# Dividing score tiles on ScalarE instead of GpSimd, in a re-ordered program with waits on the shared SBUF port

## The chip, the cores and the metric

The kernel runs on one core of a Trainium2 chip. The metric is the device time of one execution in microseconds (us), the median over several runs. The engines are TensorE (PE in the profile; PEld is its loading of the stationary operand), VectorE (DVE), ScalarE (ACT), GpSimd (POOL) and SyncE (SP). SP only issues DMAs here; POOL computes and also issues the DMAs that add to what lies in SBUF.

## The reference

One layer of a hybrid encoder trunk on x of 512 tokens by 1024 features, in float32:

```
hn  = rms_norm(x);  z = hn @ w_in                       # 1024 x 3590
o_a = 4 heads of differential attention (softmax1 - lam * softmax2) @ v, then a norm
o_b = 6 heads of attention with a cumulative log-forget-gate bias, causal
o_c = 6 heads of chunked attention with a clipped relative-position bias
h   = x + concat(o_a, o_b, o_c) @ w_out                 # 1024 x 1024
u   = causal depthwise conv of width 3 over rms_norm(h) @ w_up     # 1024 x 5632
h   = h + (silu(gate) * val) @ w_down                   # 2816 x 1024
out = h + (p @ w_ple_proj) * sigmoid(rms_norm(h) @ w_ple_gate)
```

All attention heads have 64 columns and norms on queries and keys. A softmax row is exp(s - max) divided by the sum of its exponentials. That division is what the change moves, for the heads of o_b and o_c.

## The kernel before

**Arithmetic.** A float32 product is made of three products of rounded parts: each operand is split into a high part in the format fp32r and a low part, and `mm3` (L511) issues high x high, high x low and low x high. So each weight tile is loaded by SP into `wraw`, copied on ACT to `whi`, and subtracted on DVE (for some tiles on POOL, or by an adding DMA that POOL issues) to give `wlo`. `h`, `Th` and `Tl` hold the residual and the two parts of its transposed, normed form.

**Stages.** First come the eight input projections (`in_unit`, L753), 128 tokens at a time into PSUM banks `z`, and beside them the attention of the head pairs A0, A1, B0 to B2 and C0 to C2. Then the output projection, the up-projection with the convolution (`ff_chain`, L1471), the down-projection, and the gate, whose last products run until the end. Nine of the 22 column blocks of the up-projection and all of the down-projection use a scheme with seven products in place of eight, for which POOL adds or subtracts weights.

**Attention of one head pair.** `split_q` (L715) and `split_k` (L727) turn normed columns by transposes on PE, split them on ACT and DVE, and make three moves of half a tile each on POOL (`move`, L712: `q<-q`, `q<-ql`, `k<-k`). For each head and each block of 128 queries, `softmax_map` (L852) issues two products into a bank `s`; DVE adds the bias, takes the row minimum and writes the tile `e`; ACT takes the exponential with its row sum into `st`; DVE takes the reciprocal of the sum. Then `scores` (L878) finishes the tile. For the A heads POOL scales the second map and DVE combines both. For the B and C heads (6 pairs, 2 heads, 4 blocks: 48 tiles of 128 rows and 128, 256, 384 or 512 columns) one POOL instruction multiplies `e` by the reciprocal in place (L896). `prob_cols` (L902) transposes the finished tiles on PE, and `values` (L930) multiplies them with the values.

**The order of the work.** Nothing is issued where it stands in the source. Between two calls that open and close a plan, each operation becomes an `Op` (L116) with its dependencies (`Plan.add`, L150), a duration (`Plan.price`, L184) and a due time (`Plan.due`, L225). The due time of a PE operation is its place in the PE order plus the number that `SHIFT` (L53) gives its group; those of the other engines follow backwards from what needs them. `Plan.solve` (L236) then plays all five engines against a clock and always picks the free operation that is due first. `emit` (L305) issues the operations in that order, and every engine runs its own in order. There are two plans: one for projections and attention (L595) and one for the rest (L1140).

In the play of L236, an operation on POOL, or one on DVE whose two operands lie in SBUF, is marked `port` (L216), and DVE and POOL exclude each other in such operations (`held`, L245). In the second plan a POOL operation also starts 0.1 us after the DVE operation before it (`late`), and if it is longer than 0.6 us, `emit` gives it a real semaphore wait on that DVE operation (`behind`, L362). DVE never gets such a wait, and in the first plan nobody does. Loads of SP and adding DMAs of POOL share one `wire` in the play, at 0.37 MB/us for SP's and 0.105 for POOL's (L220, L286). PE is kept from mixing single transposes with products (`STICK`, L263).

The lines of this part that matter most:

```
dve.reciprocal(st[:, 2:3], st[:, 1:2])                                          # L873
pool.tensor_scalar(e, e, st[:, 2:3], 1.0, ALU.mult, ALU.mult)                   # L896, B and C heads
if before and op.eng.name == "pool" and before.eng.name == "dve" and op.busy > self.LONG and self.late:
    op.eng.behind(op.ins, before.ins)                                           # L313
```

## Time and profile before

| | us |
|---|---|
| median of 3 runs | 708.28 (708.25 to 709.49) |
| the profiled execution | 707.89 |
| its span, first to last instruction | 706.0 |
| PE busy | 690.3 |
| DVE busy | 552.5 |
| ACT busy | 408.7 |
| POOL busy | 300.6 |

The profile is one execution. Its span is 1.9 us less than the time that was measured for the same execution. In rows of groups the columns are: line, engine, operation, what is written and read with its shapes, the count, busy us, mean ns of one, and the idle time of the engine before them with what ended it. Nearly every row has the line L357, since all operations go through one helper; so the rows are told apart by the names of the tiles. In a table of waits the columns are who waited for what, us in total, times, and the longest. In the chain of waits and the timeline they are the start, the us, and what ran; the timeline adds in brackets how long the engine was idle before and who ended that.

### The profile page before, as it was taken

What the parts mean: (1) busy time and instruction counts of PE and PEld (TensorE: products, weight loads), DVE (VectorE), ACT (ScalarE), POOL (GpSimd) and SP (SyncE); (2) the same over time, 40 slices, a digit from 0 to 9 for tenths busy, and PEclk for the clock granted to TensorE, in tenths of its full rate; (3) what the DMA queues carried; (4) which work ended last, traced back from release to release, by engine and by line L of the source; (5) the groups of instructions that cost most, each with busy time, mean ns of one, the idle gap of its engine ahead of it and who ended that gap; (6) DMA issues with size and microseconds to landing.
All of it is one profiled execution on the core that took longest, in us unless ns stands there. A gap on an engine that the chain in (4) does not pass through costs nothing.

```text
span 706.0 us, 12402 instructions
## 1 busy us (share of the span) xinstructions
PE 690.3 (98%) x4420; PEld 636.4 (90%) x4420; DVE 552.5 (78%) x1126; ACT 408.7 (58%) x781; POOL 300.6 (43%) x403
## 2 busy tenths in 40 slices
PE   7999999999999999999999999999999999999997
PEld 7999999898999888899998999889988888999886
DVE  7679878879788666789888887997877998878722
ACT  6657676565766575666666435665345674536711
POOL 3788677766665452223223334304432203245200
PEclk9999999999999999999999999999999999999999
DMA  9523444423112252584763278651488552204521
GB/s 321 201 83 111 125 117 128 118 60 109 45 61 76 75 124 83 200 244 105 214 159 113 68 186 207 163 162 33 139 211 209 183 168 82 91 32 155 163 85 46
DMA packets 41275, 92.72 MB, mean 131 GB/s; under 512 B 4694, under 2 KB 7510, under 8 KB 41212
## 3 DMA queue, kind: packets, MB, share of 16 engines
q1 hardware_dynamic: 34572, 78.24, 33.1%
q0 software_dynamic: 6352, 13.38, 10.8%
q8 instruction: 35, 0.57, 0.3%
q10 hardware_dynamic: 288, 0.30, 0.1%
q14 instruction: 28, 0.23, 0.1%
HBM read 83.63 MB, written 4.21 MB: 124 GB/s over the span
## 4 chain that ended last, share of the span: by engine, by line
PE 91%; DVE 3%; DMA 2%; ACT 2%; POOL 1%; issue 1%; ACTq 0%; POOLq 0%
PE z L357 46%; PE s L357 22%; PE t L357 16%; PE o L357 7%; DMA wraw<-in_w_up_dram 1%; DVE wlo L357 1%; POOL k L357 1%; POOL q L357 1%; ACT whi L357 1%; DMA zn<-in_w_in_dram 0%; DVE e L357 0%; DVE conv L357 0%; POOL rs L357 0%; ACT e L357 0%; DVE kl L357 0%
## 5 line engine op out<-in xcount | busy, mean ns | idle before, releaser
L357 ACT CAST whi<-wraw 128x768 fp32r<-128x768 f32 (+2 forms) x140 | 106.1, 768 | 59.9 <-POOL wraw L357 11.4
L357 PE MATMUL z<-whi,Th 128*128 128x384 f32 (+2 forms) x356 | 123.4, 351 | 4.5 <-ACT whi L357 4.5
L357 DVE TENSOR_TENSOR wlo<-wraw,whi 128x768 fp32r<-128x768 f32 (+2 forms) x122 | 111.5, 930 | 15.4 <-ACT whi L357 13.6
L357 PE MATMUL z<-wlo,Th 128*128 128x384 f32 (+2 forms) x356 | 123.0, 350 | 0.0
L357 PE MATMUL z<-whi,Tl 128*128 128x384 f32 (+2 forms) x356 | 121.8, 347 | 0.0
L357 PEld LDWEIGHTS z<-whi,Th 128*128 128x128 f32 x356 | 66.9, 189 | 8.0 <-ACT whi L357 4.5
L357 POOL TENSOR_TENSOR wraw<-wraw,wraw 128x256 f32<-128x256 f32 (+1 forms) x22 | 28.3, 1285 | 101.3 <-DVE wlo L357 53.6
L357 PEld LDWEIGHTS z<-wlo,Th 128*128 128x128 f32 x356 | 67.2, 189 | 4.0 <-DVE wlo L357 0.4
L357 PEld LDWEIGHTS z<-whi,Tl 128*128 128x128 f32 x356 | 67.0, 189 | 3.8
L357 ACT ACTIVATE e<-e,st 128x128 f32<-128x128 f32 (+3 forms) x80 | 44.7, 560 | 29.8 <-DVE st L357 29.4
L357 PE MATMUL z<-Th,whi 128*128 128x512 f32 (+1 forms) x156 | 53.2, 346 | 1.4 <-ACT whi L357 1.3
L357 PE MATMUL s<-Th,whi 128*128 128x512 f32 (+1 forms) x156 | 53.3, 345 | 0.6 <-ACT whi L357 0.6
L357 PE MATMUL s<-Th,wlo 128*128 128x512 f32 (+1 forms) x156 | 53.7, 345 | 0.0
L357 PE MATMUL s<-Tl,whi 128*128 128x512 f32 (+1 forms) x156 | 53.6, 345 | 0.0
L357 PE MATMUL z<-Tl,whi 128*128 128x512 f32 (+1 forms) x156 | 53.5, 344 | 0.0
L357 PE MATMUL z<-Th,wlo 128*128 128x512 f32 (+1 forms) x156 | 53.4, 344 | 0.0
L357 POOL TENSOR_TENSOR rs<-rs,nhalf 128x4 f32<-128x4 f32 x40 | 43.5, 1091 | 4.8 <-DVE rs L357 2.3
L357 DVE CUSTOM_DVE_ANT_0 e<-s,bias 128x128 f32<-128x128 f32 (+3 forms) x74 | 33.7, 469 | 12.4 <-PE s L357 7.2
L357 DVE TENSOR_TENSOR conv<-conv,conv 128x512 f32<-128x512 f32 (+1 forms) x31 | 21.0, 691 | 24.0 <-ACT conv L357 23.8
L357 POOL TENSOR_SCALAR e<-e,st 128x512 f32<-128x512 f32 (+3 forms) x48 | 27.2, 576 | 18.1 <-DVE st L357 16.8
L357 PEld LDWEIGHTS z<-Th,whi 128*128 128x128 f32 x156 | 29.1, 188 | 4.8 <-ACT whi L357 1.8
L357 PEld LDWEIGHTS s<-Th,whi 128*128 128x128 f32 x156 | 29.2, 188 | 3.8 <-ACT whi L357 0.8
(352 smaller groups left out, 2152.4 us busy)
## 6 DMA issues: line engine op xcount, KB each, us to landing
wraw<-in_w_up_dram SPq DMA_DIRECT2D x41, 384.0 KB, 4.3
wraw<-in_w_in_dram SPq DMA_DIRECT2D x28, 384.0 KB, 3.7
wraw<-in_w_down_dram SPq DMA_DIRECT2D x16, 384.0 KB, 3.6
whi_again<-in_w_up_dram SPq DMA_DIRECT2D x11, 384.0 KB, 4.5
wraw<-in_w_out_dram SPq DMA_DIRECT2D x16, 256.0 KB, 2.7
wlo_again<-in_w_up_dram SPq DMA_DIRECT2D x10, 384.0 KB, 4.3
wraw<-in_w_up_dram SPq DMA_DIRECT2D x15, 256.0 KB, 4.1
wlo<-wraw POOLq DMA_DIRECT2D x7, 384.0 KB, 4.2
```

The costliest lines, as they stand in the source:

```text
L357: ins = getattr(self.eng, op)(*a, **k)
```

## The change

One line of the computation changes: the 48 tiles of the B and C heads are scaled by ACT (`activation` with `Copy` and a scale per row) instead of POOL. No other instruction is added or taken away, but the order of nearly all of them may differ, as the planner is changed in these ways:

- `SHIFT`, the table of due-time shifts, has new numbers throughout.
- `emit` gives a wait on the other engine's last `port` operation to POOL and to DVE alike, in both plans, for any `port` operation longer than 0.25 us, if the play has it start before the other one's end plus 1.0 us (POOL) or 0.6 us (DVE); a wait on one that the engine already waited for is not repeated.
- In the play POOL starts 0.2 us after DVE's `port` operation and DVE 0.1 us after POOL's.
- SP's and POOL's transfers are played on two wires, at 334 and 164 KB/us alone and 143 and 78 KB/us together, with at most 8 in flight each.
- PE's rule against mixing transposes is gone, and PE prefers operations that have been free for 0.15 us in the first plan (0.1 before) and 0.1 us in the second.
- A tensor named `out_dram` is given regions like a tile's; this kernel declares its output as `out_0_dram`.

```
--- before.py
+++ after.py
@@ -51,44 +51,44 @@
 
 
 SHIFT = {
-    "first": -11.4, "in1_0": -0.3, "in1_1": -25, "in1_2": -2.7, "A0a": -6.5, "in1_3": -12.1, "in2_0": -5.9,
...
+    "first": -8.4, "in1_0": 2, "in1_1": -12, "in1_2": -0.4, "A0a": -5.7, "in1_3": -7, "in2_0": 7.3, "in2_1": 14.9,
...
 }
 
 
@@ -127,15 +127,16 @@
     WRITES = ("out", "accum_out")
     LEAD = {"act": 0.035, "dve": 0.035, "pool": 0.095, "pe": 0.055, "sp": 0.1}
 
-    def __init__(self, clock, there=(), mem=None, fresh=0.0, late=0.0):
-        self.group, self.loaded, self.fresh, self.late = "first", set(), fresh, late
+    def __init__(self, clock, there=(), mem=None, fresh=0.0, sure=0.15):
+        self.sure = sure
+        self.group, self.loaded, self.fresh = "first", set(), fresh
         self.clock, self.there, self.ops, self.mem = clock, [(v.tensor.name, self.region(v), t) for v, t in there], [], mem or {}
 
     @staticmethod
     def region(v):
         size = 2 if v.dtype == BF16 else 4
         (row, pn), *rest = [tuple(x) for x in v.ap]
-        if v.tensor.space == bass.MemoryType.DRAM and v.tensor.name not in STAND_INS:
+        if v.tensor.space == bass.MemoryType.DRAM and v.tensor.name not in STAND_INS and v.tensor.name != "out_dram":
             return 0, 1, v.offset * size, (v.offset + (pn - 1) * row + sum((n - 1) * st for st, n in rest) + 1) * size
         p0, c0 = divmod(v.offset, row)
         return p0, p0 + pn, c0 * size, (c0 + sum((n - 1) * st for st, n in rest) + 1) * size
@@ -186,7 +187,7 @@
         n = self.width(op.outs[0])
         cols = sum(1 for v in op.ins if self.width(v) == 1) - (op.name == "reciprocal")
         acc = "accum_out" in k
-        op.move, op.turns = 0, op.name == "transpose"
+        op.move = 0
         if e == "pe":
             if op.name == "transpose":
                 op.busy = 0.109
@@ -216,9 +217,10 @@
         op.port = e == "pool" and not op.move or e == "dve" and (
             len(here) == len(op.ins) and (op.name == "tensor_scalar" or op.name in ("tensor_tensor", "scalar_tensor_tensor")))
 
-    LONG, STICK = 0.6, 2.0
-    HW, SW, AT_ONCE = 0.37e6, 0.105e6, 8
-    SURE, AHEAD, MUCH, WAIT = 0.1, 1.0, 2.0, 0.6
+    SHORT, HANDED, NEAR = 0.25, {"pool": 0.2, "dve": 0.1}, {"pool": 1.0, "dve": 0.6}
+    RATE = {("sp",): {"sp": 0.334e6}, ("pool",): {"pool": 0.164e6}, ("sp", "pool"): {"sp": 0.143e6, "pool": 0.078e6}}
+    SENT, ARRIVED, AT_ONCE = {"sp": 1.46, "pool": 1.49}, 0.58, 8
+    AHEAD, MUCH, WAIT = 1.0, 2.0, 0.6
     SPARE = {"act": 1.02, "dve": 1.02, "pool": 1.05}
     ENGINES = ("dve", "pe", "act", "pool", "sp")
 
@@ -230,7 +232,7 @@
                 t += op.busy
         for op in reversed(self.ops):
             if op.eng.name != "pe":
-                spent = op.busy + op.lag + 0.05 + (op.move / self.HW + 2.0 if op.move else 0.0)
+                spent = op.busy + op.lag + 0.05 + (op.move / 0.37e6 + 2.0 if op.move else 0.0)
                 op.dl = min([q.dl for q in op.next], default=t) - spent
 
     def solve(self):
@@ -240,11 +242,47 @@
             op.left, op.at = len(op.deps), op.ready + self.LEAD[op.eng.name]
             if not op.left:
                 free[op.eng.name].append(op)
-        wire, out, order = 0.0, {"sp": [], "pool": []}, []
-        turns, alone = False, False
+        wire, now, gate, order = {"sp": [], "pool": []}, 0.0, {"sp": 0.0, "pool": 0.0}, []
         held = {"dve": 0.0, "pool": 0.0}
         other = {"dve": "pool", "pool": "dve"}
-        when = lambda q: max(q.at, held[other[q.eng.name]] + (self.late if q.eng.name == "pool" else 0.0)) if q.port else q.at
+        never = 1e18
+
+        def when(q):
+            if q.port:
+                return max(q.at, held[other[q.eng.name]] + self.HANDED[q.eng.name])
+            if q.move:
+                return max(q.at, gate[q.eng.name]) if len(wire[q.eng.name]) < self.AT_ONCE else never
+            return q.at
+
+        def release(op, e):
+            for q in op.next:
+                q.left -= 1
+                q.at = max(q.at, op.start if e == "pe" and q.eng is op.eng else op.end + self.LEAD[q.eng.name])
+                if not q.left:
+                    free[q.eng.name].append(q)
+
+        def landed(until):
+            nonlocal now
+            while now < until:
+                busy = tuple(e for e in wire if wire[e] and wire[e][0][1] <= now)
+                rate = self.RATE.get(busy, {})
+                step, who = until - now, None
+                for e in wire:
+                    if e in rate and wire[e][0][2] / rate[e] <= step:
+                        step, who = wire[e][0][2] / rate[e], e
+                    if wire[e] and e not in rate and wire[e][0][1] - now < step:
+                        step, who = wire[e][0][1] - now, None
+                now = until if step == until - now else now + step
+                for e in rate:
+                    wire[e][0][2] -= rate[e] * step
+                if who:
+                    op = wire[who].pop(0)[0]
+                    op.end = now + self.ARRIVED
+                    if len(wire[who]) + 1 >= self.AT_ONCE:
+                        gate[who] = op.end
+                    return op, who
+            return None
+
         rank = lambda q: (q.dl, q.pos)
         while True:
             best = None
@@ -253,17 +291,17 @@
                     t = max(clock[e], min(when(q) for q in free[e]))
                     if best is None or t < best[0]:
                         best = t, e
+            there = landed(best[0] if best else never) if wire["sp"] or wire["pool"] else None
+            if there:
+                release(*there)
+                continue
             if best is None:
                 break
             t, e = best
             can = [q for q in free[e] if when(q) <= t]
             if e == "pe":
-                can = [q for q in can if q.at + self.SURE <= t] or can
+                can = [q for q in can if q.at + self.sure <= t] or can
             op = min(can, key=rank)
-            if e == "pe" and op.turns != turns:
-                same = [q for q in can if q.turns == turns and q.dl < op.dl + self.STICK]
-                if same and (turns or sum(q.turns and q.dl < op.dl + self.STICK for q in can) < 2 or min(q.dl for q in same) < op.dl + self.STICK / 2):
-                    op = min(same, key=rank)
             if e not in ("pe", "sp"):
                 soon = [q for q in free[e] if t < when(q) < t + op.busy * self.AHEAD and q.dl < op.dl - self.MUCH]
                 if soon:
@@ -276,16 +314,8 @@
             free[e].remove(op)
             t0 = max(clock[e], when(op))
             busy = op.busy * (1.85 if e == "pe" and t0 < 8.6 else 1.0)
-            if e == "pe":
-                busy += 0.08 * (alone and not op.turns)
-                turns, alone = op.turns, op.turns and not turns
             if op.move:
-                done = out[e]
-                if len(done) >= self.AT_ONCE:
-                    t0 = max(t0, done[-self.AT_ONCE])
-                wire = max(t0 + 2.0, wire) + op.move / (self.HW if e == "sp" else self.SW)
-                op.end = wire + 0.6
-                done.append(op.end)
+                wire[e].append([op, t0 + self.SENT[e], op.move])
             else:
                 op.end = t0 + busy + op.lag
             op.start = t0
@@ -293,11 +323,8 @@
             if op.port:
                 held[e] = t0 + busy
             order.append(op)
-            for q in op.next:
-                q.left -= 1
-                q.at = max(q.at, op.start if e == "pe" and q.eng is op.eng else op.end + self.LEAD[q.eng.name])
-                if not q.left:
-                    free[q.eng.name].append(q)
+            if not op.move:
+                release(op, e)
         assert len(order) == len(self.ops)
         self.last = clock
         return order
@@ -306,13 +333,16 @@
         for op in self.ops:
             for d in op.deps:
                 d.next.append(op)
-        before = None
+        last, known = {"dve": None, "pool": None}, {"dve": None, "pool": None}
         for op in self.choose():
             op.ins = op.eng.now(op.name, [real(v) for v in op.a], {q: real(v) for q, v in op.k.items()})
             if op.port:
-                if before and op.eng.name == "pool" and before.eng.name == "dve" and op.busy > self.LONG and self.late:
-                    op.eng.behind(op.ins, before.ins)
-                before = op
+                e = op.eng.name
+                d = last["pool" if e == "dve" else "dve"]
+                if d and d is not known[e] and op.busy > self.SHORT and op.start < d.start + d.busy + self.NEAR[e]:
+                    op.eng.behind(op.ins, d.ins)
+                    known[e] = d
+                last[e] = op
 
     def choose(self):
         self.due(SHIFT)
@@ -893,7 +923,7 @@
                 pool.tensor_scalar(e2, e2, st2[:, 2:3], X["nlam"], ALU.mult, ALU.mult)
                 dve.scalar_tensor_tensor(e, e, st[:, 2:3], e2, ALU.mult, ALU.add)
             else:
-                pool.tensor_scalar(e, e, st[:, 2:3], 1.0, ALU.mult, ALU.mult)
+                act.activation(e, e, AF.Copy, scale=st[:, 2:3])
             PROB[pr, hh].append(e)
             if hh == 1 and qb == NT - 1:
                 KL_FREE.extend(QK[pr, part][2] for part in range(2) if (pr, part) in QK)
```

## The prediction

> **What bounds the kernel now.** I read the page's busy times first, then the stages, then who PE waited for, then the chain at those places.

> ```profile
> span 706.0 us, 12402 instructions
> PE 690.3 (98%) x4420; PEld 636.4 (90%) x4420; DVE 552.5 (78%) x1126; ACT 408.7 (58%) x781; POOL 300.6 (43%) x403
> ```

> PE is busy for 690.3 of 706.0 us. Matmuls overlap in this trace, so that is no proof that PE runs at its best, but it says that at most 15.7 us of the span are time in which PE does nothing. The table of stages tells where these are (us; PE, PEld, DVE, ACT, POOL busy with counts; clock; DMA share; GB/s).

> ```profile
> 0.00:20.00 20.00, 15.52 (x89) 15.53 (x90) 14.89 (x31) 13.32 (x25) 6.19 (x15) 1.00 0.92 332
> 100.00:150.00 50.00, 47.92 (x293) 45.75 (x292) 41.08 (x139) 31.56 (x79) 36.05 (x50) 1.00 0.37 101
> 150.00:200.00 50.00, 48.94 (x304) 46.48 (x303) 40.42 (x121) 30.86 (x74) 29.77 (x45) 1.00 0.27 84
> 330.00:380.00 50.00, 50.00 (x339) 45.98 (x338) 43.19 (x67) 30.54 (x52) 13.50 (x15) 1.00 0.62 169
> 680.00:706.00 26.00, 20.76 (x113) 17.64 (x111) 7.24 (x12) 3.70 (x6) 0.54 (x1) 0.95 0.17 56
> ```

> The first 20 us hold 4.5 us (the first load) and the last 26 hold 5.2 us (the last result on its way out). The change puts no other instruction into either, so I leave both as they are, with nothing saved and nothing lost. What is left is 15.7 - 4.5 - 5.2 = 6.0 us, mostly between 100 and 200 us; a stage of the up-projection such as 330 to 380 has none. PE's waits name the partners:

> ```profile
> engine line waited for: us in total, times, longest us
> PE z L357 <- ACT whi L357: 5.8, 2, 4.5
> PE s L357 <- POOL k L357: 2.1, 3, 1.3
> PE s L357 <- DVE st L357: 1.3, 2, 1.1
> PE s L357 <- ACT whi L357: 0.6, 1, 0.6
> PE t L357 <- DVE kl L357: 0.2, 1, 0.2
> PE t L357 <- DVE ptl L357: 0.2, 1, 0.2
> PE t L357 <- issue: 0.2, 1, 0.2
> ```

> The 4.5 us is the start. The rest is 1.3 + 2.1 + 1.3 + 0.6 + 3 x 0.2 = 5.9 us, which agrees with the 6.0. So **the most that any new order can take away is about 5.9 us, 0.8%**, while what it can add has no such limit. The work of PE itself stays: 4420 matmuls in both programs.

> **The change part by part. First, the waits that it can remove.** The chain of waits and the rows of the tiles at those places:

> ```profile
> 49.03 1.35 POOL k L357
> 121.78 1.99 POOL q L357
> 155.13 3.83 DVE wlo L357 x2
> 538.98 5.21 DMA wraw<-in_w_up_dram
> ```

> ```profile
> L357 POOL TENSOR_SCALAR q<-ql x20: 611/616/1994, 36.6 to 256.4; 64x512 fp32r<-64x512 f32 x20
> L357 POOL TENSOR_SCALAR k<-k x30: 611/616/1345, 39.2 to 257.0; 64x512 fp32r<-64x512 f32 x30
> L357 DVE TENSOR_TENSOR wlo<-wraw,whi x122: 666/951/3010, 9.5 to 645.3; 128x768 fp32r<-128x768 f32 x87, 128x512 fp32r<-128x512 f32 x31, 128x524 fp32r<-128x524 f32 x4
> 155.98 2.15 POOL L357 TENSOR_TENSOR wlo<-wraw,whi 128x768 fp32r<-128x768 f32 x1
> 138.98 0.38 PE L357 MATMUL s<-k,q 128*128 128x256 f32 x1 [0.39 <-POOL k L357]
> ```

> (Tile rows give the minimum, median and maximum in ns.) A move on POOL takes 616 ns, but one took 1994 at 121.8 us and one 1345 at 49.0; a DVE subtraction takes 951 ns, but one took 3010 at 155 us, while POOL's own subtraction of 2.15 us ran from 155.98. An engine that meets the other one on the port stands still until it is through. The 1.3 us wait for POOL at 122 us is less than the 1994 - 616 = 1.4 us that the move lost, and the 1.1 us wait for DVE lies inside the 3010 - 951 = 2.1 us that the subtraction lost. The first plan's play already excludes such pairs but nothing holds the chip to it; the new waits do, so an operation that PE waits for can be put ahead. That takes away 1.3 + 1.1 us, and at 49 us the remaining 2.1 - 1.3 - 0.39 = 0.4 us (the move lost 0.7 there). The 0.39 us wait at 139 us stands while POOL also has the first divisions; taking those from POOL removes it. **Sum of these: 3.2 us.**

> For the wire rates there is one visible place: a load with 5.21 us in the chain at 539 us, ahead of the 0.6 us wait for `whi`.

> ```profile
> wraw<-in_w_up_dram SPq DMA_DIRECT2D x41, 384.0 KB, 4.3
> wraw<-in_w_up_dram POOLq DMA_DIRECT2D x6, 384.0 KB, 5.9
> ```

> Such a load usually lands in 4.3 us from SP, so 0.9 us were lost beside others' traffic. A play that knows of it may start it earlier: between nothing and 0.6 us; I take the middle, **0.3 us**. The other wait for `whi` (1.3 us at 515 us) hangs on DVE, and I leave it.

> **Second, what it adds.** The 48 divisions leave POOL and come to ACT.

> ```profile
> L357 POOL TENSOR_SCALAR e<-e,st 128x512 f32<-128x512 f32 (+3 forms) x48 | 27.2, 576 | 18.1 <-DVE st L357 16.8 <-PE z L357 0.6 <-PE s L357 0.2
> L357 ACT ACTIVATE e<-e,st 128x512 f32<-128x512 f32 x20 | 14.4, 723 | 6.1 <-DVE st L357 5.8
> L357 ACT ACTIVATE e<-e,st 128x384 f32<-128x384 f32 x20 | 12.2, 614 | 2.7 <-DVE st L357 2.5
> L357 ACT ACTIVATE e<-e,st 128x256 f32<-128x256 f32 x20 | 10.1, 505 | 2.7 <-DVE st L357 2.7
> L357 ACT ACTIVATE e<-e,st 128x128 f32<-128x128 f32 x20 | 8.0, 400 | 18.4 <-DVE st L357 18.4
> 133.00:200.00 67.00, 65.32 (x401) 61.94 (x400) 54.75 (x182) 40.66 (x105) 41.78 (x65) 1.00 0.26 81
> 200.00:267.00 67.00, 67.00 (x378) 59.83 (x377) 50.02 (x140) 43.72 (x111) 38.40 (x62) 1.00 0.29 80
> ```

> The exponentials of the same tiles give the price: 12 x (0.400 + 0.505 + 0.614 + 0.723) = 26.9 us. The divisions lie between 133 and 267 us. ACT's busy time there goes from 40.7 + 43.7 = 84.4 to 111.3 of 134 us (63% to 83%), POOL's from 80.2 to 53.0. ACT's 49.6 us of idle time hide the 26.9, so by sum it costs nothing. But ACT runs in order, and a division that waits for its reciprocal holds up what is behind it: the evacuations `sq`, `V` and `pth`, which free PSUM for PE. In these 134 us the engine at such a load is DVE, 104.8 of 134 us (78%). PE's waits for DVE were 1.3 + 0.2 + 0.2 = 1.7 us over the whole attention, 1.1 of it from the port. So bounds for ACT at 83% are 0 (its idle time covers all) and 12 heads x 0.65 us (the mean wait of PE for `st`) = 7.8 us; I take **0.7 us**, near the DVE row without the port's share.

> The two-sided waits: with one pending on DVE, all evacuations of PSUM are queued behind it; with one on POOL, the `q` and `k` moves, the powers for `rs` and the adding DMAs. Where the partner has run, nothing is lost; a hand-over that the hardware would do anyway turns into a semaphore. No row shows one alone. Lower bound -1 us (collisions avoided that I haven't counted), upper bound in the third rival; I take **+0.3 us**. Their cover is DVE's idle time, 6.8 of 50 us between 330 and 380 us, and without that each one would be PE's.

> The lost rule on transposes costs nothing:

> ```profile
> 119.28 0.60 PE L357 MATMUL t<-ident,e 128*128 128x128 f32 x4
> 119.64 0.42 PE L357 MATMUL z<-wlo,Th 128*128 128x384 f32 x1
> 119.89 0.33 PE L357 MATMUL z<-whi,Tl 128*128 128x384 f32 x1
> ```

> From 119.28 to 119.89 us is 0.61 us for four transposes and one product; the product is worth 0.17 (its neighbours start so far apart), which leaves 0.11 for a transpose and nothing for the switch. The new `SHIFT` only permutes. `out_dram` isn't the name that this kernel declares, so that line does nothing.

> **Sum:** -3.2 - 0.3 + 0.7 + 0.3 = -2.5 us. The profiled execution took 707.89 us, of which 1.9 lie outside the span, and would come to 705.4. It stands 0.4 below the median, so against the median of 708.28 I forecast **705.8 us**.

> **The rivals.** *The waits only move the standstill.* [...] As a mechanism: a loser that waits at a semaphore loses as long as one that waits on the port, so only a better order gains, and the plan's order may be no better where PE waits. Then 0.4 us at 139 us is all that is saved, against 1.0 us added: 708.28 - 0.4 + 1.0 = 708.9 us, no change. For it: the play excluded these pairs already. Against it: three of the six waits of about 0.4 us and more lie behind standstills that the play didn't foresee.

> *ACT becomes late in attention* (slower). Each division waits for DVE's reciprocal on an engine that is 83% busy; today POOL takes this wait, 16.8 us of idle time in its row. If each of the 12 heads costs PE 0.65 us: 708.28 - 3.5 + 0.3 + 7.8 = 712.9 us. It decides once ACT's new waits exceed PSUM's slack of two banks `s`; it overtakes the gain from 5 heads on. Against it: ACT has no share in PE's waits between 100 and 200 us today.

> *DVE stands behind a late POOL* (slower). In the seven-product scheme POOL's sums wait for adding DMAs:

> ```profile
> POOL wraw L357 <- DMA wraw<-in_w_up_dram: 19.5, 7, 7.7
> ```

> A DVE operation that is planned behind such a sum now waits for that DMA too, 2.8 us on average, up to 7.7. If each of the 7 shows PE a wait like the 1.3 us one: 708.28 - 3.5 + 0.7 + 9.1 = 714.6 us. From 3 of them on the gain is eaten. Against it: split weights lie several tiles ahead, so PE sees little of one late subtraction.

> *All waits go:* 708.28 - 5.9 = 702.4 us.

> **How the numbers follow.** Chances: the forecast 0.37, all waits gone 0.07, waits only moved 0.16, ACT late 0.22, DVE behind POOL 0.18. Faster by over 0.2% (1.4 us, about what a measurement of this kernel can tell from no change) takes the first two with 0.44, within 0.2% the third with 0.16, slower the last two with 0.40. The range from 702.8 to 715.0 us leaves out most of the best case and the worse ends of the two slow ones, together under 0.2. Since both signs hold much, the forecast's own range is 703.5 to 706.9.

> **What would show it.** Right: PE's waits for `k` and `st` under 1 us together; no move on POOL over 1 us and no `wlo` on DVE over 1.5; ACT near 111 of 134 us in the division's stage and no PE wait for a tile that ACT writes. The rule of the first rival: the standstills gone, but PE's waits at the same sum. ACT late: rows PE <- ACT `e`, `pth` or `V`, or s <- DVE `st` with DVE waiting for ACT. DVE behind POOL: rows DVE <- POOL `wraw` and PE idle after 290 us. My forecast is wrong if PE's idle time outside start and end exceeds 6 us.

## The result, and the profile after

The changed kernel takes 710.09 us (median of 22 runs, 707.71 to 713.21); the kernel before, run beside it, 708.21 (22 runs, 706.51 to 710.59). The ratio is 1.0031, 95% interval 1.0020 to 1.0042: **slower by 2.2 us (1.4 to 3.0) by that ratio, where 2.5 us less had been forecast.** The profiled execution took 710.12 us. Lines that were L357 are L387 now. The page's busy times, then PE's waits (who waited for what, us in total, times, longest):

```profile
span 708.3 us, 12363 instructions
PE 694.7 (98%) x4420; PEld 639.4 (90%) x4420; DVE 542.8 (77%) x1126; ACT 431.9 (61%) x829; POOL 253.6 (36%) x355
```

```profile
PE z L387 <- ACT whi L387: 4.4, 1, 4.4
PE s L387 <- DVE st L387: 1.5, 3, 0.9
PE s L387 <- DVE wlo L387: 1.3, 2, 1.1
PE t L387 <- DVE ptl L387: 0.6, 2, 0.4
PE z L387 <- DVE wlo L387: 0.4, 1, 0.4
PE o L387 <- DVE ptl L387: 0.2, 1, 0.2
```

Outside the start PE waits 1.5 + 1.3 + 0.6 + 0.4 + 0.2 = 4.0 us, 1.9 less than before, and no longer for POOL. Yet the span is 2.3 us longer, and PE is busy 4.4 us longer with the same 4420 matmuls. So in this pair the loss is not idle time of PE but slow time. The rows of the moves and subtractions (minimum, median, maximum in ns), and of ACT's `e` (exponentials and divisions together), show that what was aimed at did happen:

```profile
L387 POOL TENSOR_SCALAR q<-ql x20: 614/617/624, 45.8 to 257.0; 64x512 fp32r<-64x512 f32 x20
L387 POOL TENSOR_SCALAR k<-k x30: 613/618/635, 47.2 to 257.6; 64x512 fp32r<-64x512 f32 x30
L387 DVE TENSOR_TENSOR wlo<-wraw,whi x122: 679/951/962, 17.0 to 647.6; 128x768 fp32r<-128x768 f32 x87, 128x512 fp32r<-128x512 f32 x31, 128x524 fp32r<-128x524 f32 x4
```

```profile
L387 ACT ACTIVATE e<-e,st 128x512 f32<-128x512 f32 x32 | 23.0, 719 | 4.6 <-DVE st L387 4.2
...
L387 ACT ACTIVATE e<-e,st 128x128 f32<-128x128 f32 x32 | 12.6, 394 | 0.8 <-DVE st L387 0.8
```

```profile
133.00:200.00 67.00, 66.66 (x413) 63.02 (x412) 57.21 (x205) 56.26 (x137) 31.42 (x48) 1.00 0.32 91
200.00:267.00 67.00, 67.00 (x385) 61.05 (x385) 50.38 (x138) 52.07 (x128) 24.79 (x38) 1.00 0.31 84
```

No move lasts over 635 ns (1994 before), no subtraction over 962 ns (3010 before). ACT is busy 56.3 + 52.1 = 108.3 of the 134 us in which the divisions lie (111.3 forecast), and PE waits for no tile that ACT writes there.

**Where the 2.3 us of this pair of profiles are.** First, the clock at the start. The timeline of PE, of before and then of after (start, us, what ran; a pair of products takes 0.84 us at half clock, 0.51 at full clock; from the start of one pair to that of the next it is 0.64 and 0.34 to 0.35 us):

```profile
6.56 0.84 PE L357 MATMUL s<-wlo,Th 128*128 128x384 f32 x2
7.20 0.57 PE L357 MATMUL z<-whi,Tl 128*128 128x384 f32 x2
7.61 0.51 PE L357 MATMUL s<-whi,Tl 128*128 128x384 f32 x2
7.95 0.51 PE L357 MATMUL z<-whi,Th 128*128 128x384 f32 x2
```

```profile
10.17 0.84 PE L387 MATMUL z<-wlo,Th 128*128 128x384 f32 x2
10.81 0.62 PE L387 MATMUL s<-wlo,Th 128*128 128x384 f32 x2
11.28 0.51 PE L387 MATMUL z<-whi,Tl 128*128 128x384 f32 x2
11.63 0.51 PE L387 MATMUL s<-whi,Tl 128*128 128x384 f32 x2
```

PE starts at 4.4 to 4.5 us in both, but full speed comes at about 7.3 us in one and 11.0 in the other. About half of that time is lost: 1.4 us before, 3.3 after. Over the 17 profiles of this study that keep one of the two orders the loss lies between 1.4 and 3.3 us, with a median of 2.6 us for the old order of attention and 2.5 for the new. These two executions are the ends of that range, so **1.9 of the 2.3 us between them are chance**. The medians of many runs should not share it, and must be explained by other things.

Second, one stretch later on. PE's waits in the timeline of after (in brackets the idle time before), then two stretches of its table of stages:

```profile
56.67 0.39 PE L387 MATMUL s<-k,q 128*128 128x256 f32 x1 [0.91 <-DVE st L387]
...
57.70 0.45 PE L387 MATMUL s<-k,q 128*128 128x384 f32 x1 [0.29 <-DVE st L387]
...
58.98 0.79 PE L387 MATMUL s<-k,q 128*128 128x512 f32 x1 [0.31 <-DVE st L387]
```

```profile
55.40:58.80 3.40, 2.07 (x11) 1.28 (x10) 3.13 (x15) 3.25 (x13) 1.95 (x4) 1.00 1.01 224
58.80:62.20 3.40, 3.22 (x11) 2.83 (x12) 3.21 (x17) 3.04 (x8) 2.86 (x5) 0.51 0.81 321
```

PE idles 1.3 of 3.4 us, and in the next 3.4 us the granted clock is 0.51: PE is "busy" for 3.22 us with 11 matmuls, where before it does 28 in the same stretch. One such step costs, as an estimate from the 3.4 us at half clock, 3.4 / 2 = 1.7 us, and shows up in no list of waits. So 1.9 + 1.7 - 1.9 (less waiting) = 1.7, near the 2.3 of this pair.

### The profile page after: what moved, and what is told of

The parts are those of the page before. It is cut to its first block, busy times and chain, and to the rows that moved or that the text cites. A ratio compares the mean times of both kernels' runs of the same rounds, so it can differ in the third digit from the quotient of the medians.

```text
span 708.3 us, 12363 instructions
## 1 busy us (share of the span) xinstructions
PE 694.7 (98%) x4420; PEld 639.4 (90%) x4420; DVE 542.8 (77%) x1126; ACT 431.9 (61%) x829; POOL 253.6 (36%) x355
## 4 chain that ended last, share of the span: by engine, by line
PE 90%; DMA 4%; DVE 2%; ACT 2%; POOL 1%; issue 1%; SPq 0%; ACTq 0%; POOLq 0%; DVEq 0%
PE z L387 47%; PE s L387 19%; PE t L387 17%; PE o L387 7%; DMA wraw<-in_w_up_dram 3%; DVE wlo L387 1%; DMA h<-in_xt_dram 0%; ACT whi L387 0%; DMA wraw<-in_w_down_dram 0%; POOL wraw L387 0%; ACT pth L387 0%; ACT sq L387 0%; POOL k L387 0%; ACT e L387 0%; DVE ptl L387 0%
## 5 line engine op out<-in xcount | busy, mean ns | idle before, releaser
L387 ACT CAST whi<-wraw 128x768 fp32r<-128x768 f32 (+2 forms) x140 | 105.4, 769 | 59.3 <-PE z L387 10.6
L387 PE MATMUL z<-whi,Th 128*128 128x384 f32 (+2 forms) x356 | 124.0, 356 | 4.4 <-ACT whi L387 4.4
L387 PE MATMUL z<-wlo,Th 128*128 128x384 f32 (+2 forms) x356 | 124.2, 355 | 0.1
L387 PE MATMUL z<-whi,Tl 128*128 128x384 f32 (+2 forms) x356 | 123.3, 352 | 0.0
L387 DVE TENSOR_TENSOR wlo<-wraw,whi 128x768 fp32r<-128x768 f32 (+2 forms) x122 | 104.8, 878 | 22.1 <-ACT whi L387 9.4
L387 ACT ACTIVATE e<-e,st 128x384 f32<-128x384 f32 (+3 forms) x128 | 68.6, 557 | 13.2 <-DVE st L387 12.3
L387 PEld LDWEIGHTS z<-whi,Th 128*128 128x128 f32 x356 | 67.3, 191 | 8.5 <-ACT whi L387 4.4
L387 PEld LDWEIGHTS z<-wlo,Th 128*128 128x128 f32 x356 | 67.3, 191 | 4.8 <-DVE wlo L387 0.8
L387 PEld LDWEIGHTS z<-whi,Tl 128*128 128x128 f32 x356 | 67.2, 190 | 4.1 <-issue 0.2
L387 PE MATMUL z<-Th,wlo 128*128 128x512 f32 (+1 forms) x156 | 53.5, 345 | 0.4 <-DVE wlo L387 0.4
L387 PE MATMUL z<-Th,whi 128*128 128x512 f32 (+1 forms) x156 | 53.9, 346 | 0.0
L387 PE MATMUL z<-Tl,whi 128*128 128x512 f32 (+1 forms) x156 | 53.6, 344 | 0.0
L387 PE MATMUL s<-Tl,whi 128*128 128x512 f32 (+1 forms) x156 | 53.3, 346 | 0.0
L387 PE MATMUL s<-Th,whi 128*128 128x512 f32 (+1 forms) x156 | 53.1, 345 | 0.0
L387 PE MATMUL s<-Th,wlo 128*128 128x512 f32 (+1 forms) x156 | 52.9, 345 | 0.0
L387 POOL TENSOR_TENSOR wraw<-wraw,wraw 128x256 f32<-128x256 f32 (+1 forms) x22 | 28.1, 1283 | 62.4 <-DVE wlo L387 53.2
L387 POOL TENSOR_TENSOR rs<-rs,nhalf 128x4 f32<-128x4 f32 x40 | 40.5, 1017 | 10.8 <-DVE wlo L387 6.4
L387 DVE CUSTOM_DVE_ANT_0 e<-s,bias 128x128 f32<-128x128 f32 (+3 forms) x74 | 33.9, 470 | 6.9 <-PE s L387 5.9
L387 DVE TENSOR_TENSOR conv<-conv,conv 128x512 f32<-128x512 f32 (+1 forms) x31 | 20.2, 670 | 21.4 <-ACT conv L387 20.4
L387 PEld LDWEIGHTS z<-Th,wlo 128*128 128x128 f32 x156 | 29.2, 188 | 4.0 <-DVE wlo L387 0.7
L387 PEld LDWEIGHTS z<-Th,whi 128*128 128x128 f32 x156 | 29.2, 188 | 3.6 <-ACT whi L387 0.3
L387 PEld LDWEIGHTS s<-Tl,whi 128*128 128x128 f32 x156 | 29.3, 188 | 3.5
## 6 DMA issues: line engine op xcount, KB each, us to landing
wraw<-in_w_up_dram SPq DMA_DIRECT2D x41, 384.0 KB, 4.1
wraw<-in_w_in_dram SPq DMA_DIRECT2D x28, 384.0 KB, 3.8
wraw<-in_w_down_dram SPq DMA_DIRECT2D x16, 384.0 KB, 3.0
whi_again<-in_w_up_dram SPq DMA_DIRECT2D x11, 384.0 KB, 4.2
wlo_again<-in_w_up_dram SPq DMA_DIRECT2D x10, 384.0 KB, 4.5
wlo<-wraw POOLq DMA_DIRECT2D x7, 384.0 KB, 4.4
```

The costliest lines, as they stand in the source:

```text
L387: ins = getattr(self.eng, op)(*a, **k)
```

## The experiments

After the result I held **theory W**: a new wait on DVE near 50 us dries PE out at 55 to 59 us and so causes the half-clock step. Rivals were the division's new engine, the new order of attention, and the new order of the rest (up- and down-projection). Letters in an expectation stand for the theories that it states.

**The waits.** In one kernel only POOL's waits on DVE are kept in the changed one (the edit below). In the other the line that sets a wait is left out, so that every wait on the port is gone, also those of POOL in the second plan, whose like the kernel before has by its old rule. The order stays.

```
-                if d and d is not known[e] and op.busy > self.SHORT and op.start < ...:
+                if e == "pool" and d and d is not known[e] and op.busy > self.SHORT and op.start < ...:
```

> The changed kernel in its own order, with GpSimd's waits on VectorE but without VectorE's waits on GpSimd. Theory W: as with no waits at all, about 707 us, since it is VectorE's wait that starves PE. Rivals S and D: 709.5 to 710.5.

Measured 710.93 us, ratio to before 1.0041 (1.0028 to 1.0053): the changed kernel's time. The waits at 55 to 59 us are still there (0.57, 0.38 and 0.31 us). **Theory W fell**, and DVE's waits cost and give nothing that can be measured here.

> The changed kernel in its own order of issue, without any of the new waits between VectorE and GpSimd on the port. Theory W (one of these waits holds VectorE idle for 4.1 us at 50 us, PE then runs dry at 55 to 59 us and gets half its clock for 3.4 us): the 4.1 us wait, most of PE's 1.5 us of waits at 55 to 59 us and the stretch of half clock go, and the median is about 707 us, 3 below the changed kernel's 710.1. Rival S (the new order of issue costs the time, the waits nothing): 709.5 to 710.5. Rival D (the division on ScalarE costs it): 709.5 to 710.5 too. Without the waits some operations should meet on the port again and last over 1.5 us.

Measured 733.26 us, 1.0351 (1.0325 to 1.0376). So POOL's waits are worth 22 us to this order. Most of that is not a gain of the new rule: between 20 and 267 us PE idles 4.6 us (2.4 with POOL's waits), between 267 and 680 us it idles 19.1 (2.6), and there the waits of the old rule do as well (710.94 us, the last run below). The rows of this kernel say what happens without them:

```profile
L386 DVE TENSOR_TENSOR wlo<-wraw,whi x122: 677/951/8493, 16.1 to 672.3; 128x768 fp32r<-128x768 f32 x87, 128x512 fp32r<-128x512 f32 x31, 128x524 fp32r<-128x524 f32 x4
```

```profile
PE t L386 <- DVE h L386: 8.9, 3, 7.0
```

One DVE subtraction takes 8.5 us (the median is 951 ns), from 643.7 us, while POOL works without a break from 644.1 to 651.4, and PE waits for DVE.

**The division alone.** Each order is kept and only the engine of the 48 divisions swapped: on POOL in the changed kernel, on ACT in the kernel before.

```
-                act.activation(e, e, AF.Copy, scale=st[:, 2:3])
+                pool.tensor_scalar(e, e, st[:, 2:3], 1.0, ALU.mult, ALU.mult)    # issued where the order has it
```

> The changed kernel with its own order and waits, but the 48 divisions are issued on GpSimd at their places in the order. Theory W: unchanged, 709.5 to 711, as the loss lies ahead of the first division. Rival D: 1.5 to 2.5 us faster, about 708. Rival S: unchanged.

Measured 716.43 us, 1.0111 (1.0095 to 1.0128); PE's waits have a new row:

```profile
PE t L391 <- POOL e L391: 2.0, 4, 1.0
```

> The kernel before with its own order and waits, but the 48 divisions are issued on ScalarE at their places in the order. Theory W and rival S: within 1 us of the kernel before, 707.5 to 709. Rival D: 2 us slower, about 710.

Measured 713.27 us, 1.0072 (1.0059 to 1.0086); PE's new rows:

```profile
PE o L361 <- ACT pth L361: 1.0, 3, 0.5
PE t L361 <- ACT e L361: 1.0, 2, 0.8
```

Each order was made for its engine: the other engine costs 5 to 6 us either way (0.0072 x 708 = 5.1; (1.0111 - 1.0031) x 708 = 5.7). The 5.7 us hold something else too: moved to POOL in this way, the divisions get no waits on DVE, and two of them took 1.6 and 2.1 us (medians 0.37 and 0.70). "ACT becomes late" is a real mechanism where the order is not made for it; its rows show 2.0 of the 5.1 us.

**The planner's inputs.** Here a rule is changed and the program planned anew: the old rule on transposes put back, one shift changed, and the division moved in the kernel before with its old `SHIFT`.

```
-    "in2_1": 14.9, "A0b": 3.6, "in2_2": 4, "A0s01": 25, ...
+    "in2_1": 14.9, "A0b": 3.6, "in2_2": 4, "A0s01": -25, ...
```

> The changed kernel with one number of the due-time table set back: A0s01 from 25 to -25, so that the first score products of the pair A0 are spread ahead of the projection's end instead of following it in one burst at 55 to 59 us. Theory B (the burst leaves PE without other work there, which costs 1.5 us of waits and, in some runs, 1.7 us of half clock): PE is not idle between 50 and 62 us, and the time falls by 1.5 to 3 us, to about 708. Rival (the plan pushes the same idle time to a later place of the attention): 709.5 to 711, PE's waits in the first 200 us as large as before.

> The changed kernel with PE's old rule against mixing single transposes and products put back, and the order planned anew. If the mixing costs time: 1 to 4 us faster, and fewer than 20 single transposes between products (51 in the changed kernel, 3 in the one before). If a single transpose costs no more than one in a run: within 1 us of 710, apart from what the other order does to the waits.

> The kernel before with the division alone moved to ScalarE, and the order of issue planned anew for it by the planner of before with its old due-time table. If ScalarE at 83% of its time is too late in attention (second rival of the prediction): 711 to 714, with PE waits for tiles that ScalarE writes. If the division costs nothing where the order is planned for it: 707.5 to 709.5. The version in the old order took 713.3.

Measured 731.93 us (1.0344, 1.0330 to 1.0358), 720.22 (1.0186, 1.0165 to 1.0207) and 726.36 (1.0274, 1.0253 to 1.0296). One of the 267 numbers in `SHIFT` costs 22 us. So a new plan with shifts that were fitted to another one tells of the fit, not of the rule; these three runs decide nothing on the parts, but they show how much hangs on the order. From here on the orders were kept fixed.

**Repeats**, to see what of the two profiles is chance.

> The changed kernel once more, unaltered, for a second profile. Theory G (what a profile shows of the clock differs from run to run: full clock is granted on a grid of 3.41 us whose place is chance, so the start costs 1.4 to 3.3 us, and a stretch in which PE runs dry may or may not cost a step of half clock): the first full clock and the places of half clock differ from those of the first profile, while PE's waits for other engines stay within 1 us of 4.0 us in sum outside the start. Rival: the clock follows the program, and the second profile shows full clock at 11.0 us and half clock at 58.8 us again. Time 709 to 711 either way.

> The kernel before once more, for a second profile. If its part after attention is as steady as theory M needs: PE loses between 3 and 5 us from 300 to 700 us again, and no stretch of half clock lies between 20 and 690 us. If it is as unsteady as the changed kernel's: 5 us or more, with waits for whi.

Measured 709.81 us (706.82 to 714.21; ratio 1.0031, 1.0014 to 1.0049) for the changed kernel, and 707.83 in one run for the one before. The second profile of the kernel before idles 0.8 us between 300 and 700 us (2.0 in the first), with no step at half clock. The changed kernel's second profile has the full clock at 59 us but stands at 437 to 440, in the up-projection, and is at half clock after that:

```profile
436.40:439.80 3.40, 1.48 (x10) 1.01 (x8) 2.87 (x4) 2.92 (x4) 0.76 (x1) 1.00 1.00 183
439.80:443.20 3.40, 3.18 (x11) 2.79 (x12) 2.78 (x4) 1.10 (x2) 0.00 (x0) 0.55 0.85 300
```

The place of the slow clock differs between executions, then, as theory G has it. But PE's waits outside the start come to 7.2 us there, not to 4.0 +- 1: how late the weights come differs from execution to execution as well.

**The halves exchanged.** The first plan of one kernel with the second plan's order and waits of the other.

```
+    def emit_frozen(self):      # the second plan's order and waits, read from a list
+        order, behind = FROZEN[len(self.ops)]
+        for op in [self.ops[int(p)] for p in order.split()]:
```

> The changed kernel's first plan (attention, division on ScalarE, two-sided waits) followed by the rest in the order and with the waits of the kernel before. Theory M (the attention of the changed kernel is no slower; the time is lost in the up-projection, where split weights come late in the new order): 706.5 to 708.5, the same as or a little faster than the kernel before, and no long PE waits for whi or wlo near 438 us. Rival A (the attention part costs it): 709.5 to 711, like the changed kernel.

Measured 708.64 us, 1.0006 (0.9994 to 1.0018): the time of before, and not faster either.

> The mirror image: the first plan of the kernel before, followed by the rest in the order and with the waits of the changed kernel. Theory M: 709.5 to 712, as slow as the changed kernel or slower, with PE's waits for whi and wlo at about 437 and 545 us. Rival A: 707.5 to 709, like the kernel before.

Measured 712.02 us, 1.0050 (1.0031 to 1.0070). **The loss comes with the new order of the rest.** The stages 430 to 450 and 540 to 580 us of before, of after, and of the new attention with the old rest (us; PE, PEld, DVE, ACT, POOL busy; clock; DMA share; GB/s):

```profile
430.00:450.00 20.00, 20.00 (x131) 18.10 (x130) 16.57 (x24) 11.90 (x20) 6.26 (x8) 1.00 0.79 208
...
540.00:580.00 40.00, 39.43 (x250) 35.35 (x249) 35.88 (x58) 25.78 (x42) 4.72 (x7) 1.00 0.61 183
```

```profile
430.00:450.00 20.00, 18.88 (x118) 16.61 (x118) 15.90 (x25) 10.63 (x17) 6.23 (x8) 1.00 0.85 213
...
540.00:580.00 40.00, 39.45 (x227) 34.00 (x226) 33.94 (x52) 23.53 (x38) 6.77 (x9) 1.00 0.63 179
```

```profile
430.00:450.00 20.00, 20.00 (x135) 18.25 (x134) 16.32 (x24) 12.65 (x22) 6.52 (x9) 1.00 0.76 206
...
540.00:580.00 40.00, 40.00 (x255) 35.98 (x255) 36.53 (x59) 27.20 (x43) 5.56 (x7) 1.00 0.63 185
```

The old rest does 131 and 135 matmuls in the first stretch, the new one 118. Behind the new attention, the new rest costs (1.0031 - 1.0006) x 708 = 1.8 us.

**The new waits without the new order.** The kernel before with the new rule of waits, in both plans and then in the first only.

```
+                if not self.late:        # the first plan; without this line, both
+                    d = last["pool" if e == "dve" else "dve"]
+                    if d and d is not known[e] and op.busy > 0.25 and op.start < d.start + d.busy + {"pool": 1.0, "dve": 0.6}[e]:
+                        op.eng.behind(op.ins, d.ins)
```

> The kernel before in its own order, with the new rule for waits on the port: both engines, both plans, over 0.25 us. If waits in both directions and in attention pay for themselves: 1 to 3 us faster than the kernel before, 705 to 707, with PE's waits behind stretched GpSimd moves gone. If they only move the standstill: 707.5 to 709. If VectorE's waits hurt: 710 or more.

Measured 706.31 us, 0.9979 (0.9970 to 0.9987).

> The kernel before with the new rule of waits in the first plan only (both engines); the second plan keeps the old waits. The run with the rule in both plans took 706.3 us. If the gain is that of the removed standstills in attention, this takes 706.3 +- 0.5 as well; if the second plan's new waits carry part of it, it lies between 706.8 and 708.2.

Measured **705.43 us, 0.9957 (0.9945 to 0.9970): 3.0 us less than before, and the fastest whole kernel of the study**. In the second plan the new waits give nothing, and perhaps cost a little (0.9979 against 0.9957). In the first they keep the moves on POOL to their time:

```profile
L364 POOL TENSOR_SCALAR q<-ql x20: 612/614/618, 37.9 to 255.8; 64x512 fp32r<-64x512 f32 x20
L364 POOL TENSOR_SCALAR k<-k x30: 611/616/628, 40.7 to 257.2; 64x512 fp32r<-64x512 f32 x30
```

**Why the new rest is slow.** The chain of waits of the changed kernel ahead of the stop at 439 us:

```profile
428.89 6.82 DMA wraw<-in_w_up_dram
...
435.81 0.63 ACT whi L387
...
437.67 1.83 DVE wlo L387 x2
439.50 0.04 issue
439.55 0.74 PE s L387 x4
```

An adding DMA that POOL issues at 428.89 lands 6.8 us later; the split on ACT and DVE follows, and PE stands until 439.55. Theory L says that weights land with no time to spare; theory C, that the order of DVE, ACT and POOL is late by itself. To tell them apart all 27 adding DMAs are cut short, in both kernels; this leaves three quarters of each of these sums of weights out of the computation.

```
-            pool.dma_start(out=w.t[:, c0:c1], in_=src(), accum_op=ALU.add)
+            n = (c1 - c0) // 4
+            pool.dma_start(out=w.t[:, c0 : c0 + n], in_=src()[:, :n], accum_op=ALU.add)
```

> The changed kernel with its order and waits as they are, but each adding DMA of the seven-product scheme moves only the first quarter of its columns (that part of the weight sums is left out; nothing else). Theory L (the re-ordered rest loses because its weight loads land with no time to spare): with transfers that take less time, PE's waits for whi and wlo near 437 us and in 540 to 580 us go, PE is busy 20.0 of 20 us in 430 to 450, and the time falls by 2 to 3 us to about 707 us, while the same cut in the kernel before changes it by under 1 us. Theory C (the order of DVE, ACT and POOL itself is the cause, not the transfers): the time stays within 1 us of 710.1.

> The kernel before with the same cut: each adding DMA of the seven-product scheme moves a quarter of its columns, order and waits unchanged. Theory L: within 1 us of 708.2, since before has slack there; its small waits at 515 and 540 us (1.9 us together) are the most that can go. Theory C says the same of this run; the two differ in the changed kernel.

Measured 705.50 us for the changed kernel (0.9964, 0.9952 to 0.9976) and 706.32 for the one before (0.9971, 0.9961 to 0.9981), both against the whole kernel before. The changed one gains (1.0031 - 0.9964) x 708 = 4.7 us, the other 2.1, more than expected (so loads cost the kernel before some time as well). **With short transfers the difference is gone**, so theory L holds. The stages of the changed kernel with short adds are full:

```profile
430.00:450.00 20.00, 20.00 (x127) 17.92 (x126) 17.47 (x27) 12.91 (x20) 6.97 (x9) 1.00 0.76 219
...
540.00:580.00 40.00, 40.00 (x238) 35.24 (x237) 36.72 (x57) 24.21 (x38) 4.85 (x7) 1.00 0.57 170
```

The kernels with whole transfers say the same. Between 290 and 580 us ACT waits 5 to 9 times for the landing of a weight that it copies to `whi` in the five profiles with the old rest in the table below, and 10 to 13 times in the five with the new one. What the runs do not tell is whether the new order issues these transfers later or needs them sooner.

Then single adding DMAs are cut, first one and then four. The expectations mean the one of 428.9 us, but the edit cuts the next one, of 768 columns, which the changed kernel issues at 431.94 us:

```
+            if op.pos == 1495:
+                k["out"], k["in_"] = k["out"][:, :192], k["in_"][:, :192]
```

POOL's adding DMAs issued from 421 to 432 us, in the changed kernel and then with the cut (the two of 256 KB are those of 421.87 and 428.89):

```profile
wraw<-in_w_up_dram POOLq DMA_DIRECT2D x2, 256.0 KB, 6.0
wraw<-in_w_up_dram POOLq DMA_DIRECT2D x1, 384.0 KB, 8.4
```

```profile
wraw<-in_w_up_dram POOLq DMA_DIRECT2D x2, 256.0 KB, 5.0
wraw<-in_w_up_dram POOLq DMA_DIRECT2D x1, 96.0 KB, 4.3
```

> The changed kernel with one adding DMA alone cut to a quarter: the one issued at 428.9 us, which took 6.8 us in the chain of waits ahead of PE's standstill at 437 to 440 us. If that one transfer is what PE waits for there, 430 to 450 us shows PE busy 19.6 us or more (18.9 now) and the time falls by 1 to 2 us to about 708.5. If the wait is set by the operations around it, nothing changes.

Measured 710.84 us, 1.0027 (1.0014 to 1.0040): no gain that can be measured. The stages, and then one line of the chain and the stop behind it:

```profile
430.00:450.00 20.00, 20.00 (x130) 18.10 (x129) 17.54 (x27) 12.72 (x20) 6.97 (x9) 1.00 0.86 234
...
540.00:580.00 40.00, 37.72 (x221) 32.59 (x222) 34.53 (x53) 23.39 (x38) 5.84 (x8) 1.00 0.63 178
```

```profile
530.80 8.01 DMA whi_again<-in_w_up_dram
```

```profile
541.33 0.38 PE L528 MATMUL s<-xh,whi 128*128 128x256 f32 x1 [1.66 <-ACT whi L528]
```

In this profile the stop at 439 us is gone, and PE stands 2.3 us in 540 to 580 (0.6 and 1.6 in the two profiles of the changed kernel), most of it behind another adding DMA, whose landing took 8.0 us. Whether the cut took the stop away is not shown, as the next run has the same cut there and keeps the stop.

> The changed kernel with 4 of its 27 adding DMAs of the up-projection cut to a quarter of their columns: the one issued at 428.9 us and the three issued between 541 and 551 us, which stand in the chain ahead of the two places where PE waits. If those two places are the whole loss, PE is busy 20.0 of 20 us in 430 to 450 and over 39.8 of 40 in 540 to 580, and the time comes to 706 +- 0.8, nearly that of all 27 cut (705.5). If the tightness is everywhere, the wait moves to a third place and the time stays above 708.

Measured 708.91 us, 1.0008 (0.9995 to 1.0022), some 1.6 us less than the changed kernel by the ratios, but not the 706 of "two places are all". That is no test of the two places, since the DMAs ahead of them are whole: its profile still idles 1.4 us in 430 to 450 behind the 256 KB of the chain above (6.82 us from 426.21 here) and 1.5 us at 544 behind an adding DMA of 533.83 that took 7.62 us. So these two runs show only that a few short transfers bring little (none measurable, then 1.6 us), where all 27 bring 4.7.

> The changed kernel's order throughout, but in the second plan only the old rule's waits (37 waits of POOL behind DVE in place of 87 of both); the first plan keeps the new ones. If the new waits in the rest delay the issue of adding DMAs, this gains 1 to 2 us on the changed kernel (708.3 to 709.1) and PE's waits for whi and wlo after 430 us shrink. If the order alone is late, it stays at 709.5 to 710.5; if the waits are what keeps the order on the chip, it is slower than 711.

Measured 710.94 us, 1.0038 (1.0023 to 1.0053). So it is the order of the rest and not its new waits that brings the weights late.

What the profiles of the kernels with whole transfers say in one table: PE's idle time in two spans (their length less PE's busy time in the table of stages), and steps at half clock after 20 us.

| order of attention, of the rest | PE idle 20-267 us | PE idle 267-580 us | half-clock steps |
|---|---|---|---|
| before, before (two profiles) | 4.0, 3.8 | 2.0, 0.8 | none |
| before with new waits in both; in the first plan | 2.0; 2.1 | 1.2; 0.2 | none |
| after, before | 2.7 | 2.1 | none |
| after, after (two profiles) | 2.6, 2.6 | 1.7, 4.9 | at 59; at 440 |
| after, after without DVE's waits; with old waits in the rest | 2.4; 2.7 | 2.6; 4.0 | both at 440 |
| before, after | 4.1 | 3.4 | none |

## Why the prediction was wrong

**The waits removed, -3.2 us: right as a mechanism.** No move or subtraction stands still any more (at most 635 and 962 ns), and in the order before the new waits alone give -3.0 us (2.1 to 3.9), PE's idle time in attention falling from 3.9 to 2.1. The other 1.2 us are not explained: in that one profile the rest, whose waits are the old ones, idles 0.2 us instead of 2.0 and 0.8. All the same it speaks against the first rival in attention: at the same order the waits at semaphores cost PE 3.9 - 2.1 = 1.8 us less than the standstills that they replaced. The size was wrong for the changed kernel. It gets 3.9 - 2.6 = 1.3 us, since its own order has new waits for `st` at 55 to 59 us (1.5 us); the prediction said `k` and `st` under 1 us together, and `st` alone is 1.5.

**The division on ACT, +0.7 us: nothing of it seen.** Price (394 to 719 ns) and load (108.3 us) were right, and the second rival didn't come in an order that was planned for it. In one that wasn't, it costs 5.1 us. No run tests the lost rule on transposes by itself, which the prediction put at nothing.

**The two-sided waits, +0.3 us:** DVE's cost nothing in the changed kernel (710.93 without them). The third rival's signs did come: the changed kernel has a row DVE `wlo` <- POOL `wraw` of 4.3 us in 6 waits, and PE idles after 290 us. Its mechanism did not carry the loss, as without DVE's waits the time is the same. The place that it named, adding DMAs after 290 us, was where the time went, by another way.

**The step that failed** is the one that priced the rest of the program: "A play that knows of it may start it earlier: between nothing and 0.6 us; I take the middle, 0.3 us", and "The new `SHIFT` only permutes." That term takes the rest as it stands, with no loss possible. In its place, by the table: PE's idle time in 267 to 580 us is 1.3 on average over the five rows of the old order (2.0, 0.8, 1.2, 0.2, 2.1) and 3.3 over the five of the new one (1.7, 4.9, 2.6, 4.0, 3.4), +2.0 us (of the 2.1, 1.2 lie at a seam, see below); three of those five also have a step at half clock there, 3 x 1.7 / 5 = +1.0. So **+3.0 us where -0.3 stood**. In time, the new rest costs 3.5 us (2.2 to 5.0) behind the old attention and 1.8 behind the new. What failed beside it is the size of the first term, -1.3 where -3.2 stood. With -1.3 from attention and its half-clock step at 59 us, which one of the eight profiles with the new attention shows (1.7 / 8 = 0.2), -1.3 + 0.2 + 3.0 = +1.9, against 2.2 measured. These are few profiles, so each term is good to about 1 us, and the third is rather too large: the five profiled executions of the new rest were 1.0 us slower, on average, than the medians of their kernels.

The new attention with the old rest measured +0.4 us (-0.4 to 1.3), where -1.3 might be expected. Most of the gap lies at the seam of the two plans, where PE waits in that kernel for DVE's `h`, which comes after the last `oall` and `Tl` of the attention in the chain of waits:

```profile
280.87 0.50 PE L525 MATMUL z<-whi,Th 128*128 128x512 f32 x1 [1.17 <-DVE h L525]
```

Neither the kernel before nor the changed one waits there. With it, -1.3 + 1.2 = -0.1, inside the interval.

**"The work of PE itself stays"** failed too, in a smaller way: the matmuls stay, but PE's speed does not (11 matmuls in 3.4 us at a granted clock of 0.51, where before does 28). Half-clock time counts as busy, so the prediction's own test (idle time over 6 us outside start and end) says nothing in the first profile, with 4.3 us; in the second, with 7.5, it does.

Whether the first rival is right in the rest, so that a wait taken away there comes back at another place, is not shown, as no run shortens the one DMA ahead of a stop. Nor is it shown which part of the planner makes the new order tight. The new wire rates are the suspect, but plans with one rule changed came out 10 us and more slower for want of fitted shifts, so the rates alone could not be tried.

## What to carry to other kernels

A change that orders a program anew is not priced by the operations that it moves: ask for each stage that was without waits how much time its loads have to spare, as the new order can take that away where nothing seemed to be changed. Where one part of a change has a clear mechanism, try it in the old order by itself; here the waits alone, in attention alone, gave 3.0 us and the whole change cost 2.2. To learn what late loads are worth, shorten all of them at once, and to try a single one, make sure by its size and time of issue that the edit has hold of the one in the chain.

## What the runs showed of the hardware

**Between DVE and POOL it was POOL's waiting that counted.** In the changed kernel's order POOL's waits behind DVE save 22 us (733.26 us without any, 710.93 with POOL's alone), most of it in the second plan, and DVE's waits behind POOL nothing measurable (710.09 with both).
